# An expert backbone on one core: up matrices in runs of 8192 bytes, token rows stored in the order of the gather

## The chip, the cores and the metric

The kernel runs on one core of one Trainium2 chip. The metric is the device time of one execution in microseconds (us). Three runs of the kernel before are given, with their median; beside them stands one execution that was profiled.

The engines are called by the names of the profile: PE (TensorE, with PEld for its loads of the stationary operand), DVE (VectorE), ACT (ScalarE), POOL (GpSimd) and SP (SyncE, which here only issues transfers). One core has 16 DMA engines.

## What is computed

Two layers of a diffusion backbone on 256 latent and 256 context tokens of width 1024, all in float32. Each layer has a mixer (Fourier mixing, differential attention, a recurrent unit), and then a mixture of 32 experts, of which each token takes two. The change lies in the experts:

```python
def _hier_moe(xt, w_group, b_group, w_router, b_router, w1, w3, w2):
    # w1, w3: (32, 1024, 512), w2: (32, 512, 1024)
    ...                                  # group, then the two best experts of the group
    def body(acc, blk):
        e, toks, ws = blk
        xb = xpad[toks]
        hb = jax.nn.silu(xb @ w1[e]) * (xb @ w3[e])
        yb = (hb @ w2[e]) * ws[:, None].astype(xb.dtype)
        return acc.at[toks].add(yb), None

for l in range(DEPTH):                   # DEPTH = 2
    ...                                  # x (and in layer 0 also the context) through the mixer
    hx2 = _adaln(x, norm2_g[l], sh2, sc2).reshape(B * S, D)
    y = _hier_moe(...)                   # layer 0: 512 tokens; layer 1: the 256 latent ones
    x = x + g2 * y.reshape(B, S, D)
```

Every expert is loaded in full in either layer: 2 MB each of w1, w3 and w2, so 192 MB a layer.

## The kernel before

A token tile has 128 tokens: four tiles in layer 0, two in layer 1. For each layer `mixer` and `proj_prep` run, and then `moe`. The order of the instructions on each engine is the order in which the code is written.

**Loads.** All weights go through one list, `stream`, from which `issue` (L169) takes the next load, gets a slot `S()` of 128 x 2048 floats (22 of them) and issues the transfer on SP (L177). `issue` is called as slots come free; SP then waits for the slot's last reader. A load of an expert is half a matrix, 1 MB: for w1 and w3 512 rows of 512 floats, for w2 256 rows of 1024. `pairs` (L194) puts two neighbouring rows side by side in a partition:

```python
return ap.rearrange("(j p i) f -> p j (i f)", p=128, i=2)
```

For w2 there is one `j`, so that a partition gets 2 x 1024 floats in one piece, 8192 bytes. For w1 and w3 there are two, each of 2 x 512 floats: two pieces of 4096 bytes that lie 128 x 4096 bytes apart in memory. The experts go in units: a unit is one expert with up to 64 tokens, or two experts with up to 32 each. The loads of a unit come in the order w1 and w3 of the first half, w1 and w3 of the second, w2. The first three experts (18 loads) are fixed and are loaded ahead; for the others SP reads the expert's number from the routing (L222).

**Token rows.** `stage_a` to `stage_d` of `proj_prep` make a tile's normed rows in `buf` (128 tokens x 1024 channels): `stage_a` on DVE and ACT, with a small operation on POOL (L162) for the root, `stage_b` on DVE (L1166, two operations of 512 elements), `stage_c` on PE with copies on ACT (transposes, and the logits of the routing). `stage_d` (L1183) splits the rows into two parts for the gather: ACT casts them to `hh` (L1189), POOL subtracts (L1190) to get the rest, `hl`. The order written out is: `stage_d` of the tile before the last follows `stage_b` of the last. Behind the last `stage_c` stands the routing, a chain of small DVE operations from L1235 on, which ends in the one-hot tables (L1386).

**Gather and experts.** `gather` (L1393) multiplies `hh` and `hl` as stationary operands with the one-hot tables, and so gets the tokens of a unit with channels on partitions. Since a partition of a w1 load holds rows 2m and 2m + 1 of a block of 256, the stationary operand must be every second channel: `hsl` (L1373) takes it through `odd` (L1369), with a step of two floats. `up` (L1446) multiplies with w1 and w3, `act` makes the hidden values, `hid_t` transposes them, `down` (L1470) multiplies with w2, `combine` (L1485) brings the result back to the tokens. `overflow` with `block` (L1498) is for tokens that don't fit in the units; it runs a loop whose count comes from the routing.

Of the kernel before, what the change touches and what calls it, by code (L numbers as in the profile page):

```python
# [17 lines left out]
D = 1024  # L18
# [51 lines left out]
def tile_backbone(  # L70
# [27 lines left out]
    V, A, G, PE, SP = nc.vector, nc.scalar, nc.gpsimd, nc.tensor, nc.sync  # L98
# [19 lines left out]
    def f(ap):  # L118
        return ap.bitcast(FT)
# [35 lines left out]
    ident = ca[:, IDENT:IDENT + 128]  # L155
# [9 lines left out]
    stream = []  # L165
# [3 lines left out]
    def issue(n):  # L169
        while state["issued"] < min(n, len(stream)):  # L170
            key, src, kk = stream[state["issued"]]
            if callable(src):
                src = src()
            t = S()
            dst = t[:, 0:2048].rearrange("p (k f) -> p k f", k=kk)
            for i, one in enumerate(src if isinstance(src, list) else [src]):
                SP.dma_start(dst[:, i * one.shape[1]:(i + 1) * one.shape[1]], one)  # L177
            loaded[key] = t
            state["issued"] += 1

# [10 lines left out]
    def kp(ap):  # L191
        return ap.rearrange("(k p) f -> p k f", p=128)

    def pairs(ap):  # L194

        return ap.rearrange("(j p i) f -> p j (i f)", p=128, i=2)

    def s_mod(l, n):
        for h in range(2):
# [17 lines left out]
    def expert(l, rank, w):  # L217

        if rank < FIXED[l]:
            return w[l, rank]  # L220
        if (l, rank) not in picked:
            picked[l, rank] = nc.values_load(  # L222
                by_rank[l][0:1, rank:rank + 1], engines=(ET.SP,), min_val=0, max_val=NE - 1,
                skip_runtime_bounds_check_because="the ranks are a permutation of the experts")
        return w[l, bass.DynSlice(picked[l, rank], 1)].rearrange("o a f -> (o a) f")

    def s_exp(l, ranks):
        for h in range(2):
            for e in ranks:
                stream.append((("w1", l, e, h), lambda e=e, h=h: pairs(expert(l, e, w1)[h * 512:(h + 1) * 512, :]), 2))  # L230
                stream.append((("w3", l, e, h), lambda e=e, h=h: pairs(expert(l, e, w3)[h * 512:(h + 1) * 512, :]), 2))
        for h in range(2):
            for e in ranks:
                stream.append((("w2", l, e, h), lambda e=e, h=h: pairs(expert(l, e, w2)[h * 256:(h + 1) * 256, :]), 1))

    def s_experts(l):
        at = len(stream)
# [824 lines left out]
    def proj_prep(l, mixh, mixl, raw, pre, ends):  # L1062
# [34 lines left out]
        ws = dict(enumerate(pre))  # L1097
# [45 lines left out]
        hh, hl = [], []  # L1143
        buf = S()
# [38 lines left out]
        def stage_d(i):  # L1183

            o = slice(i % 2 * D, (i % 2 + 1) * D)
            if i % 2 == 0:
                hh.append(S(FR))
                hl.append(S(FR))
            A.copy(hh[i // 2][:, o], buf[:, o])  # L1189
            G.tensor_sub(hl[i // 2][:, o], buf[:, o], f(hh[i // 2][:, o]))  # L1190

        for i in range(nt):
            p = pz[i] if l else PS()
# [65 lines left out]
        for i in range(2):  # L1259
            m = c1[2 + i]  # L1260
# [13 lines left out]
        key, rank = scratch(32), scratch(32)  # L1274
# [87 lines left out]
    def moe(l, r):  # L1362
        tts, nt, hh, hl = r["tts"], r["nt"], r["hh"], r["hl"]
# [5 lines left out]
        def odd(ap, k):  # L1369

            return ap.rearrange("p (j m i) -> p j m i", m=128, i=2)[:, k // 2, :, k % 2]

        def hsl(t, i, d):  # L1373
            return odd(t[i // 2][:, (i % 2) * D:(i % 2 + 1) * D], d)

        ohs, xts, wss, ots = {}, {}, {}, {}

# [120 lines left out]
        def block(rc, wc, ws, tiles):  # L1498
            o, ot, y1, s0, s1, x2, x3, pa, pb, pd = tiles
            y0 = o  # L1500
            for i in range(nt):
                ov = o[:, i * 128:(i + 1) * 128].rearrange("p (b h s) -> p b h s", b=2, h=2)
                for h in range(2):
                    V.tensor_tensor(out=ov[:, :, h], in0=iota[:, None, :].to_broadcast([128, 2, 32]),
                                    in1=rc[:, h, i:i + 1][:, :, None].to_broadcast([128, 2, 32]), op=OP.is_equal)
            spin(BS[0], hh[0], pb)

            n = 0
            for i in range(nt):
                for t in (hh, hl):  # L1510
                    for h in range(2):
                        c = (i % 2) * D + h * 512
                        mm((pa, pd)[h], o[:, i * 128:(i + 1) * 128], t[i // 2][:, c:c + 512],
                           n == 0, n == 2 * nt - 1)
                    n += 1
            A.copy(s0[0:64, :], pa[0:64, :])
            V.tensor_copy(s0[64:128, :], pd[64:128, :])
            spin(BS[1], hh[0], pb)
            for k in range(4):
                PE.transpose(pd[:, k * 128:(k + 1) * 128], odd(s0, k), ident)  # L1520
                if k == 1:
                    A.copy(s1[:, 0:256], pd[:, 0:256])
            V.tensor_copy(s1[:, 256:512], pd[:, 256:512])
            up(0, lambda k: s1[:, (k % 4) * 128 + (k // 4) * 64:(k % 4) * 128 + (k // 4 + 1) * 64], [ws], pa)
            for i in range(nt):
                PE.transpose(pb[:, i * 128:(i + 1) * 128], f(o[:, i * 128:(i + 1) * 128]), ident)
            spin(BS[2], hh[0], pd)
            for h in range(2):
                c = slice(h * 256, (h + 1) * 256)
                A.activation(s0[0:64, c], pa[0:64, c], AF.Silu)  # L1530
                V.tensor_mul(s0[0:64, c], s0[0:64, c], pa[64:128, c])
                for k in (2 * h, 2 * h + 1):
                    PE.transpose(pd[:, k * 64:(k + 1) * 64], odd(s0[0:64, :], k), ident[0:64, 0:64])
            A.copy(s1[:, 0:256], pd[:, 0:256])
            V.tensor_copy(ot[:, 0:nt * 128], pb[:, 0:nt * 128])
            down(s1, [ws], pa[0:64, :], pa[64:128, :])
            spin(BS[3], hh[0], pd)

            for h, y in enumerate((y0, y1)):
                a = 64 * h  # L1540
                A.copy(y[a:a + 64, :], pa[a:a + 64, :])
                V.tensor_sub(y[64 - a:128 - a, :], pa[a:a + 64, :], f(y[a:a + 64, :]))
            xs = s0, s1, x2, x3
            for n in range(2 * nt):
                h, i = n // nt, n % nt
                tt, p, t = tts[i], (pb, pd, pa)[n % 3], xs[n % 4]
                mm(p, ot[:, i * 128:(i + 1) * 128], (y0, y1)[h], True, True)
                c = slice(h * 512, (h + 1) * 512)
                gg = (D if tt < 2 else 0) + h * 512
                V.scalar_tensor_tensor(t, p, wc[:, 0, i:i + 1], g2[:, gg:gg + 512], op0=OP.mult, op1=OP.mult)  # L1550
                ADD(n, 2 * nt).tensor_add(xr_(tt, c), xr_(tt, c), t)

        def overflow():
# [3 lines left out]
            with tc.If(v > 0):  # L1557
# [21 lines left out]
                ws = {k: [S(), S()] for k in ("w1", "w3", "w2")}  # L1579
# [3 lines left out]
                with tc.For_i(0, v, 1):  # L1583

                    V.reduce_max(top, rem, axis=AX.X)
                    V.tensor_tensor(out=one, in0=rem, in1=top.to_broadcast([128, 32]), op=OP.is_equal)
                    V.tensor_tensor(out=one, in0=one, in1=t32, op=OP.mult)
                    V.reduce_max(code, one, axis=AX.X)
                    V.tensor_tensor(out=one, in0=t32, in1=code.to_broadcast([128, 32]), op=OP.is_equal)
                    V.tensor_scalar(top, code, -1.0, 32.0, op0=OP.mult, op1=OP.add)  # L1590
                    V.tensor_copy(eid, top[0:1])
                    e = nc.values_load(eid, engines=(ET.SP,), min_val=0, max_val=NE - 1,
                                       skip_runtime_bounds_check_because="the place of a maximum among the experts")
                    for key, w, rows, kk in (("w1", w1, 512, 2), ("w3", w3, 512, 2), ("w2", w2, 256, 1)):
                        for h in range(2):
                            SP.dma_start(ws[key][h].rearrange("p (k f) -> p k f", k=kk),
                                         pairs(w[l, bass.DynSlice(e, 1)].rearrange("o a f -> (o a) f")[h * rows:(h + 1) * rows, :]))
                    for o, a in ((rc, rme), (wc, wte)):
                        V.tensor_tensor(out=prod, in0=a, in1=oneb, op=OP.mult)
                        V.reduce_sum(o[:, 0], prod, axis=AX.X)  # L1600
                    V.tensor_scalar(rc[:, 1], rc[:, 0], -32.0, None, op0=OP.add)
                    V.scalar_tensor_tensor(rem, one, -64.0, rem, op0=OP.mult, op1=OP.add)
                    V.scalar_tensor_tensor(rme, oneb, -64.0, rme, op0=OP.mult, op1=OP.add)
                    block(rc, wc, ws, tiles)
# [191 lines left out]
```

## Time and profile before

| | us |
|---|---|
| runs (3): median, lowest, highest | 1519.53, 1518.34, 1521.59 |
| the profiled execution, whole | 1518.4 |
| its span in the trace | 1516.5 |
| PE busy | 1301.8 (86%) |
| PEld busy | 684.3 (45%) |
| DVE busy | 617.9 (41%) |
| ACT busy | 366.1 (24%) |
| POOL busy | 360.0 (24%) |

Times within the trace count from the start of the span. Layer 0 runs to about 820 us, its experts from about 341 us; layer 1's experts run from about 1044 us to the end. A slice of the page is 37.9 us. [...]

### The profile page before, as it was taken

Reading aid. Unit: us, or ns where it says so; the run is one execution under the profiler, and the core shown is the slowest. Engines: PE = TensorE matmul, PEld = TensorE weight load, DVE = VectorE, ACT = ScalarE, POOL = GpSimd, SP = SyncE. Lnnn points to the kernel's source line nnn. Section 1 sums busy time; section 2 is a strip of 40 time slices with the busy share of each in tenths; the row PEclk is TensorE's granted clock in tenths of the full one; section 3 lists DMA queues with packets and bytes.
Section 4 is the critical chain, followed back from the end, with each engine's and each line's share of the span. In section 5 each row is a group of like instructions: output and inputs, shape, how many; then the busy total and the mean of one; then the engine's idle time right before and its main releaser. Section 6 shows DMA issues by size and latency. Waiting matters only on the chain. (4 is left out here: it accounts for less than half of the span.)

```text
span 1516.5 us, 18764 instructions
## 1 busy us (share of the span) xinstructions
PE 1301.8 (86%) x6910; PEld 684.3 (45%) x6910; DVE 617.9 (41%) x1209; ACT 366.1 (24%) x757; POOL 360.0 (24%) x396
## 2 busy tenths in 40 slices
PE   5989987969999897989898999787989878897775
PEld 3767544755545352535352776375334223231221
DVE  3587586562343322232223678875122111110111
ACT  3433664322111010101012544741111001010000
POOL 2333012420252222222222651141111111100110
PEclk9999999989999998999998999998999989889898
DMA  9943362275999999999999924184999999999996
GB/s 340 388 149 121 116 220 76 84 305 235 413 414 410 414 412 413 412 414 412 413 412 389 376 86 139 37 336 187 412 414 413 413 414 411 413 414 413 413 413 253
DMA packets 134266, 489.66 MB, mean 323 GB/s; under 512 B 10411, under 2 KB 13081, under 8 KB 117785
## 3 DMA queue, kind: packets, MB, share of 16 engines
q1 hardware_dynamic: 129520, 485.11, 81.1%
q10 hardware_dynamic: 4649, 3.29, 0.9%
q8 instruction: 56, 0.92, 0.2%
q14 instruction: 41, 0.34, 0.1%
HBM read 487.32 MB, written 1.05 MB: 322 GB/s over the span
## 5 line engine op out<-in xcount | busy, mean ns | idle before, releaser
L125 PE MATMUL ps<-s 128*32 128x512 f32 (+3 forms) x2488 | 532.7, 615 | 92.3 <-DMA s<-in_w 88.3
L125 PEld LDWEIGHTS ps<-s 128*32 128x32 f32 (+2 forms) x2488 | 173.4, 138 | 409.1 <-issue 222.2
L1496 POOL TENSOR_TENSOR xres<-xres,w 128x512 f32<-128x512 f32 x92 | 116.4, 1292 | 429.1 <-DVE w L1495 429.1
L1460 DVE SCALAR_TENSOR_TENSOR w<-w,ws,ps 64x512 f32<-64x512 f32 x48 | 35.9, 747 | 413.6 <-ACT w L1459 413.6
L125 PE MATMUL ps<-s,ht 128*32 128x512 f32 (+1 forms) x1056 | 178.8, 596 | 8.9 <-ACT ht L1467 7.2
L125 PE MATMUL ps<-w,s 128*128 128x512 f32 x672 | 168.9, 404 | 1.3 <-POOL w L526 0.6
L1459 ACT ACTIVATE w<-ps 64x512 f32<-64x512 f32 x48 | 28.4, 592 | 569.0 <-PE ps L125 569.0
L1496 POOL TENSOR_TENSOR s<-s,w 128x512 f32<-128x512 f32 x50 | 63.2, 1287 | 373.5 <-DVE w L1495 373.5
L125 PEld LDWEIGHTS ps<-w,s 128*128 128x128 f32 x672 | 127.6, 193 | 34.2 <-issue 4.4
L526 POOL TENSOR_TENSOR w<-s,w 128x512 fp32r<-128x512 f32 x80 | 110.4, 1391 | 122.2 <-ACT w L525 104.8
L1495 DVE TENSOR_TENSOR w<-ps,s 128x512 f32<-128x512 f32 x148 | 91.0, 681 | 71.3 <-PE ps L125 71.2
L125 PE MATMUL ps<-s,w 128*128 128x512 f32 (+2 forms) x480 | 101.3, 361 | 6.0 <-DVE s L519 3.2
L125 PEld LDWEIGHTS ps<-s,ht 128*32 128x32 f32 (+1 forms) x1056 | 50.7, 122 | 114.0 <-issue 99.6
L125 PE MATMUL ps<-w 128*128 128x512 f32 (+1 forms) x392 | 89.9, 381 | 2.5 <-ACT w L1481 1.4
L125 PEld LDWEIGHTS ps<-s,w 128*128 128x128 f32 x480 | 75.5, 198 | 35.3 <-issue 12.3
L1482 DVE TENSOR_TENSOR w<-ps,w 128x512 fp32r<-128x512 f32 x48 | 30.9, 686 | 135.2 <-ACT w L1481 135.2
L125 PE MATMUL ps<-oh,s 128*128 128x256 f32 (+1 forms) x640 | 84.0, 293 | 0.0
L125 PEld LDWEIGHTS ps<-oh,s 128*128 128x128 f32 x640 | 81.6, 205 | 3.2 <-issue 2.4
L125 PEld LDWEIGHTS ps<-w 128*128 128x128 f32 x392 | 67.1, 197 | 35.2 <-issue 18.0
L125 PE MATMUL ps<-s,cond 128*32 128x512 f32 x336 | 55.4, 645 | 0.0
L1408 DVE COPY s<-ps 128x512 f32<-128x512 f32 (+1 forms) x26 | 16.9, 649 | 93.2 <-PE ps L125 93.2
L525 ACT CAST w<-s 128x512 fp32r<-128x512 f32 x80 | 48.3, 620 | 4.3 <-issue 1.4
(260 smaller groups left out, 1131.7 us busy)
## 6 DMA issues: line engine op xcount, KB each, us to landing
s<-in_w SPq DMA_DIRECT2D x384, 1024.0 KB, 19.4
s<-in_w_mod SPq DMA_DIRECT2D x48, 1024.0 KB, 12.7
s<-in_w_in SPq DMA_DIRECT2D x18, 1024.0 KB, 14.9
s<-in_w_out SPq DMA_DIRECT2D x8, 512.0 KB, 6.6
s<-in_w_out SPq DMA_DIRECT2D x4, 1024.0 KB, 7.9
s<-in_const_b SPq DMA_DIRECT2D x2, 768.0 KB, 14.8
s<-in_xc SPq DMA_DIRECT2D x2, 512.0 KB, 4.7
xres<-in_x SPq DMA_DIRECT2D x2, 512.0 KB, 8.0
```

What stands on the lines that cost most here:

```text
L125: PE.matmul(o, l, r, start=start, stop=stop)
L525: A.copy(wh[:, 0:n], src)
L526: G.tensor_sub(wl[:, 0:n], src, f(wh[:, 0:n]))
L1408: (V.tensor_copy if dd % 2 else A.copy)(v3(xt[:, dd * 512:(dd + 1) * 512], 256)[:, :, 0:m * 128], v3(ps, 256)[:, :, 0:m * 128])
L1459: A.activation(sh[a:a + 64, :], ps[a:a + 64, :], AF.Silu)
L1460: V.scalar_tensor_tensor(sh[a:a + 64, :], sh[a:a + 64, :], ws, ps[64 - a:128 - a, :], op0=OP.mult, op1=OP.mult)
L1482: V.tensor_sub(yl, ps, f(yh))
L1495: V.tensor_tensor(out=t, in0=ps, in1=g2[:, gg:gg + 512], op=OP.mult)
L1496: (V if end and h else G).tensor_add(xr_(tt, c), xr_(tt, c), t)
```

## The change

`pairs` gives way to `runs`: a partition gets four neighbouring rows of w1 or w3, 8192 bytes in one piece. For w2 the result is what it was. For the up matrices channel `4m + i` of a half then sits in partition m, at place i. `stage_d` therefore writes `hh` and `hl` in that order: for each half of 512 channels first all m with i = 0, then i = 1, and so on. It reads `buf` with a step of four floats and writes without a step, and it does so in two casts and two subtractions for a tile where there was one of each. `hsl` takes 128 neighbouring floats. The hidden values still use `odd`, since w2 lies as before. In `block`, the gathered rows come in the new order, so that their transposes need no step.

```diff
-            dst = t[:, 0:2048].rearrange("p (k f) -> p k f", k=kk)
+            dst = t[:, 0:2048].rearrange("p (k f) -> p k f", k=kk) if kk else t[:, 0:2048]
...
-                SP.dma_start(dst[:, i * one.shape[1]:(i + 1) * one.shape[1]], one)
+                SP.dma_start(dst[:, i * one.shape[1]:(i + 1) * one.shape[1]] if kk else dst, one)
...
-    def pairs(ap):
-
-        return ap.rearrange("(j p i) f -> p j (i f)", p=128, i=2)
+    def runs(ap):
+
+        return ap.rearrange("(p i) f -> p (i f)", p=128)
...
-                stream.append((("w1", l, e, h), lambda e=e, h=h: pairs(expert(l, e, w1)[h * 512:(h + 1) * 512, :]), 2))
+                stream.append((("w1", l, e, h), lambda e=e, h=h: runs(expert(l, e, w1)[h * 512:(h + 1) * 512, :]), 0))
...
-            A.copy(hh[i // 2][:, o], buf[:, o])
-            G.tensor_sub(hl[i // 2][:, o], buf[:, o], f(hh[i // 2][:, o]))
+            b4 = buf[:, o].rearrange("p (h m i) -> p h i m", h=2, i=4)
+            h4, l4 = [t[i // 2][:, o].rearrange("p (h i m) -> p h i m", h=2, i=4) for t in (hh, hl)]
+            for h in range(2):
+                A.copy(h4[:, h], b4[:, h])
+                G.tensor_sub(l4[:, h], b4[:, h], f(h4[:, h]))
...
         def hsl(t, i, d):
-            return odd(t[i // 2][:, (i % 2) * D:(i % 2 + 1) * D], d)
+            a = (i % 2) * D + d * 128
+            return t[i // 2][:, a:a + 128]
...
-                PE.transpose(pd[:, k * 128:(k + 1) * 128], odd(s0, k), ident)
+                PE.transpose(pd[:, k * 128:(k + 1) * 128], s0[:, k * 128:(k + 1) * 128], ident)
```

The lines for w3 and w2 in `s_exp`, and the loads in `overflow`, change like that of w1.

On SP, the second unit's loads of layer 0 stand so before (a name with a number is a buffer, `in_w1` and the like are the matrices in memory):

```order
L177 DMA s_2742<-in_w1 128x2x1024
L177 DMA s_2744<-in_w3 128x2x1024
L177 DMA s_2746<-in_w1 128x2x1024
L177 DMA s_2748<-in_w3 128x2x1024
L177 DMA s_2750<-in_w2 128x2048
L177 DMA s_2752<-in_w2 128x2048
```

and so in the changed kernel:

```order
L177 DMA s_2750<-in_w1 128x2048
L177 DMA s_2752<-in_w3 128x2048
L177 DMA s_2754<-in_w1 128x2048
L177 DMA s_2756<-in_w3 128x2048
L177 DMA s_2758<-in_w2 128x2048
L177 DMA s_2760<-in_w2 128x2048
```

The order is the same; the up matrices' transfers have the shape of w2's.

On POOL, at the end of layer 0's `proj_prep` (`n2r` holds the roots of a tile, `s_2473` and `s_2614` the parts `hl`, `s_2391` is `buf`), before:

```order
L1190 TENSOR_TENSOR s_2473<-s_2391,s_2472 128x1024
L162 TENSOR_TENSOR n2r_2192<-n2r_2192,ca_72 128x1 x2
L1190 TENSOR_TENSOR s_2614<-s_2391,s_2613 128x1024 x2
L1496 TENSOR_TENSOR s_70<-s_70,w_3027 128x512
L1496 TENSOR_TENSOR s_70<-s_70,w_3033 128x512
```

and in the changed kernel:

```order
L1193 TENSOR_TENSOR s_2473<-s_2391,s_2472 128x512 x2
L162 TENSOR_TENSOR n2r_2192<-n2r_2192,ca_72 128x1 x2
L1193 TENSOR_TENSOR s_2618<-s_2391,s_2617 128x512 x4
L1500 TENSOR_TENSOR s_70<-s_70,w_3035 128x512
L1500 TENSOR_TENSOR s_70<-s_70,w_3041 128x512
```

Nothing moved past anything else; each subtraction became two of half the size, and on ACT each cast likewise.

## Rows read from the trace of the kernel before

**Rows 1.** The page: GB/s of 40 slices; shares of the chain of waits, by engine.

```profile
GB/s 340 388 149 121 116 220 76 84 305 235 413 414 410 414 412 413 412 414 412 413 412 389 376 86 139 37 336 187 412 414 413 413 414 411 413 414 413 413 413 253
...
PE 19%; DMA 18%; DVE 4%; ACT 2%; issue 1%; POOL 1%; SPq 0%; DVEq 0%; ACTq 0%; POOLq 0%
```

**Rows 2.** Table of stretches: stretch, length, busy us (instructions) by engine, clock, DMA share, GB/s.

```profile
360.00:520.00 160.00, 154.08 (x916) 72.87 (x916) 55.22 (x89) 23.05 (x48) 50.36 (x40) 1.00 1.02 411
...
520.00:815.00 295.00, 263.94 (x1452) 120.69 (x1456) 76.92 (x131) 34.82 (x75) 70.16 (x57) 0.95 1.02 412
...
1060.00:1500.00 440.00, 361.80 (x1927) 125.19 (x1928) 71.01 (x131) 42.19 (x93) 49.66 (x40) 0.92 1.02 412
```

**Rows 3.** Table of stretches, loads of w2 alone: the highest and the lowest rate.

```profile
1201.00:1207.00 6.00, 6.00 (x38) 1.66 (x32) 0.74 (x1) 0.59 (x1) 0.00 (x0) 1.00 1.02 423
...
1292.00:1298.00 6.00, 5.50 (x25) 1.34 (x26) 0.00 (x0) 0.00 (x0) 0.00 (x0) 0.50 1.01 416
```

**Rows 4.** Table of stretches, loads of w1 and w3 alone: the highest and the lowest rate.

```profile
628.00:642.00 14.00, 13.52 (x78) 6.63 (x78) 6.72 (x11) 1.55 (x3) 9.93 (x8) 1.00 1.03 411
...
1136.00:1151.00 15.00, 14.48 (x74) 5.55 (x67) 3.77 (x6) 1.49 (x4) 4.22 (x4) 1.00 1.02 407
```

**Rows 5.** DMA traffic of 1201 to 1207, 628 to 642, 357 to 800, 1060 to 1502.

```profile
DMA packets 347, 2.54 MB, mean 423 GB/s; under 512 B 37, under 2 KB 37, under 8 KB 37
...
DMA packets 1493, 5.75 MB, mean 411 GB/s; under 512 B 91, under 2 KB 91, under 8 KB 1492
...
DMA packets 39990, 182.46 MB, mean 412 GB/s; under 512 B 2772, under 2 KB 2772, under 8 KB 32701
...
DMA packets 39566, 181.37 MB, mean 410 GB/s; under 512 B 2768, under 2 KB 2768, under 8 KB 32118
```

**Rows 6.** Expert loads by tile, issue to landing: 357 to 815, then 1060 to 1502.

```profile
DMA to landing us min/median/max: 7.0/19.4/20.7
...
DMA to landing us min/median/max: 6.1/20.0/21.2
```

**Rows 7.** PE's waits (total us, times, longest): 370 to 860, then 1040 to 1516.

```profile
PE ps L125 <- DMA s<-in_w: 27.5, 17, 6.8
...
PE ps L125 <- DMA s<-in_w: 62.4, 53, 4.6
```

**Rows 8.** Timeline of PE (start, us, work, [idle before]): last waits of both layers.

```profile
798.29 1.04 PE L125 MATMUL ps<-s 128*32 128x512 f32 x2 [1.40 <-DMA s<-in_w]
...
800.84 1.08 PE L125 MATMUL ps<-s 128*32 128x512 f32 x4 [1.50 <-DMA s<-in_w]
...
1502.20 1.06 PE L125 MATMUL ps<-s,ht 128*32 128x512 f32 x8 [0.81 <-DMA s<-in_w]
```

**Rows 9.** Timelines of POOL and DVE, end of `proj_prep` in layers 0 and 1.

```profile
317.39 2.34 POOL L1190 TENSOR_TENSOR s<-s 128x1024 fp32r<-128x1024 f32 x1
...
317.42 2.85 DVE L1166 SCALAR_TENSOR_TENSOR s<-s,n2r 128x512 f32<-128x512 f32 x1 [0.66 <-POOL n2r L162]
...
320.20 0.74 DVE L1166 SCALAR_TENSOR_TENSOR s<-s,n2r 128x512 f32<-128x512 f32 x1
...
1031.66 0.34 DVE L1248 TENSOR_TENSOR w<-w 128x8 f32<-128x8 f32 x1
...
1032.03 0.17 DVE L1249 TENSOR_TENSOR w<-w,ca 128x8 f32<-128x8 f32 x1
```

**Rows 10.** Groups by shape: total us, mean ns of one, idle before them.

```profile
L1189 ACT CAST s<-s 128x1024 fp32r<-128x1024 f32 x6 | 6.3, 1043 | 0.0
...
L1115 ACT CAST s<-s 128x512 fp32r<-128x512 f32 x16 | 9.3, 621 | 0.0
...
L1496 POOL TENSOR_TENSOR xres<-xres,w 128x512 f32<-128x512 f32 x92 | 116.4, 1292 | 429.1 <-DVE w L1495 429.1
...
L125 PEld LDWEIGHTS ps<-oh,s 128*128 128x128 f32 x640 | 81.6, 205 | 3.2 <-issue 2.4
...
L125 PEld LDWEIGHTS ps<-w,s 128*128 128x128 f32 x672 | 127.6, 193 | 34.2 <-issue 4.4 <-POOL w L526 1.4 <-POOL s L904 0.8
```

More of the change, by code (lines that the diff above doesn't have):

```diff
@@ L229, in s_exp @@
             for e in ranks:
-                stream.append((("w1", l, e, h), lambda e=e, h=h: pairs(expert(l, e, w1)[h * 512:(h + 1) * 512, :]), 2))
-                stream.append((("w3", l, e, h), lambda e=e, h=h: pairs(expert(l, e, w3)[h * 512:(h + 1) * 512, :]), 2))
+                stream.append((("w1", l, e, h), lambda e=e, h=h: runs(expert(l, e, w1)[h * 512:(h + 1) * 512, :]), 0))
+                stream.append((("w3", l, e, h), lambda e=e, h=h: runs(expert(l, e, w3)[h * 512:(h + 1) * 512, :]), 0))
         for h in range(2):
             for e in ranks:
-                stream.append((("w2", l, e, h), lambda e=e, h=h: pairs(expert(l, e, w2)[h * 256:(h + 1) * 256, :]), 1))
+                stream.append((("w2", l, e, h), lambda e=e, h=h: runs(expert(l, e, w2)[h * 256:(h + 1) * 256, :]), 0))
     def s_experts(l):
@@ L1593, in overflow @@
                                        skip_runtime_bounds_check_because="the place of a maximum among the experts")
-                    for key, w, rows, kk in (("w1", w1, 512, 2), ("w3", w3, 512, 2), ("w2", w2, 256, 1)):
+                    for key, w, rows in (("w1", w1, 512), ("w3", w3, 512), ("w2", w2, 256)):
                         for h in range(2):
-                            SP.dma_start(ws[key][h].rearrange("p (k f) -> p k f", k=kk),
-                                         pairs(w[l, bass.DynSlice(e, 1)].rearrange("o a f -> (o a) f")[h * rows:(h + 1) * rows, :]))
+                            SP.dma_start(ws[key][h][:, 0:2048],
+                                         runs(w[l, bass.DynSlice(e, 1)].rearrange("o a f -> (o a) f")[h * rows:(h + 1) * rows, :]))
                     for o, a in ((rc, rme), (wc, wte)):
```

## The prediction

> **What bounds the kernel now.** I read the page's slices first: from the eleventh slice to the twenty-first, and again from the twenty-ninth to the thirty-ninth, the DMA moves 410 to 414 GB/s in every slice, and nowhere else does it for long [rows 1]. These are the two expert stages, one per layer. The chain of waits says the same of layer 1 (it can't be followed back into layer 0, which is why its shares make half of the span): 18% of the span is DMA beside 19% TensorE [rows 1]. Then the table of stretches: the mean share of the DMA engines is 1.02 from 360 to 815 us and from 1060 to 1500 us, while TensorE (PE) has 31 us to spare in the 295 us after 520 and 78 in the 440 us after 1060 [rows 2]. In 360 to 520 us PE is busy 154 of 160 us, so there alone it keeps pace with the DMA. So both expert stages are as long as their bytes take, and what counts is the rate.
>
> That rate isn't one number. Twelve short stretches in which nearly all packets are of 8192 bytes (the down matrices w2) run at 416 to 423 GB/s, with a mean by length of 419.8; the highest and the lowest are shown [rows 3]. Fourteen stretches in which all packets are of 4096 bytes (w1 and w3) run at 407 to 411, mean 409.3; again the highest and the lowest are shown [rows 4]. That they are what I call them is seen in the packet counts: in 1201 to 1207 us only 37 of 347 packets are under 8 KB, and these 37 are the small ones under 512 B; in 628 to 642 us 1492 of 1493 are under 8 KB, 1401 of them above 2 KB [rows 5]. The engines are full in both (share 1.02 and 1.03), so the difference of 2.6% is what a longer packet is worth. It can't be that something else waits.
>
> **The change part by part.** (1) The up matrices. A load of 1 MB went as 256 packets of 4096 bytes and will go as 128 of 8192, 8 KB in a row to each partition. A load of w2 is already just that, 1 MB in one piece and 8 KB to a partition, by the same queue, from the same memory, so I take its rate for the new one. What is affected are the 4 KB packets inside the two full stretches: 32701 - 2772 = 29929 from 357 to 800 us, and 32118 - 2768 = 29350 from 1060 to 1502 us [rows 5]. That is 122.6 MB and 120.2 MB. At 409.3 GB/s they take 299.5 and 293.7 us, at 419.8 GB/s 292.0 and 286.4: **7.5 us less in layer 0 and 7.3 in layer 1, 14.8 together.** The first 18 loads of either layer, which come before the stretches, meet idle engines and save nothing. Bounds: with the worst of one kind and the best of the other (411 against 416) 3.6 + 3.5 = 7.1 us, with 409.3 against 423 9.7 + 9.5 = 19.2 us. I take the means, since they rest on 67 and 205 us.
>
> Does the gain reach the end? In layer 1 PE waits for expert loads 53 times and 62.4 us in all [rows 7], the last time at 1502 us for the last load [rows 8], so the end moves with the DMA. In layer 0 it waits 17 times, 27.5 us [rows 7], and the last two waits, 1.4 and 1.5 us for up matrices, end at 798.3 and 800.8 us, at the last up products of the layer [rows 8]. The end of PE's row is the latest of (landing + the work behind it) over all loads; the last wait binds now, and every wait before it has the later waits as slack, 2.9 us and more, against a gain that differs by 0.017 us for each microsecond between them. So the whole 7.5 us should come through. The queue must not run dry either: the shortest time from issue to landing is 7.0 us in layer 0 and 6.1 in layer 1, the median 19.4 and 20.0 [rows 6]. Around 440 us, where the 7.0 stands, the DMA will be ahead by only about 1.4 us. The small loads of layer 1's projections follow in the same queue and shift along with it.
>
> (2) The token rows' parts. Each of the six calls of `stage_d` (four tiles in layer 0, two in layer 1) makes two casts on ScalarE (ACT) and two subtractions on GpSimd (POOL) of 512 elements, reading with a step of 16 bytes, where one of 1024 without a step stood. No row of before has such a step on either engine. What it touches is VectorE (DVE): before the last tile of layer 0, POOL's subtraction (2.34 us from 317.39) and DVE's L1166 start together, and L1166 takes 2.85 us, where its next one takes 0.74 [rows 9]; it waits until POOL is done. This pair of L1166, 2.85 + 0.74 = 3.6 us less a small overlap, so 3.5, is on the way to the routing, the first gather, and so to the moment at which expert loads flow freely. In layer 1 the same happens, and there a small DVE operation, L1248, also waits until the last subtraction ends (0.34 us, where the next of its kind takes 0.17) [rows 9].
>
> Let h be the time of one half on POOL. The nearest rows are 1.17 us (half of 2.34) and 1.29 us (a 512-element addition on POOL without a step) [rows 10]; the far end is 2.34, as if the step doubled each element's time. The pair now ends 2.34 us (POOL) and some 1.2 us of its own work after the start. If DVE and POOL take turns, it ends at 2h + 1.2, so 2h - 2.3 us later than now; if DVE gets both of its operations through after the first half, h - 2.3. The last subtraction of a layer can start after a cast of 0.62 us instead of 1.04 [rows 10], and ends 2h - 2.34 - 0.42 = 2h - 2.8 us later than now; so L1248 moves back by nothing for h up to 1.4, and by 1.9 us for 2.34. Over both layers that is -2.4 us at best, +0.5 for 1.29 with turns, and 2 x (2.4 + 1.9) = +8.6 at the far end. I take 0, by the nearer rows, and keep both ends. If ACT's casts doubled too, POOL would start some 0.4 us later, another +0.8.
> [...]
>
> (3) The gather reads its weights without a step. Its 640 weight loads take 205 ns each, others of that shape 193 [rows 10]; they lie beside matmuls, and only the two first gathers (64 and 32 loads) are on the path. 96 x 12 ns = 1.2 us at most; I take 0. The overflow block, which is edited too, isn't executed: no row of its lines is in the trace.
>
> Sum: -14.8 + 0 + 0. The profiled execution took 1518.4 us, 1516.5 of them its span, so 1503.6 by its clock; it lies 1.1 us below the median of the runs, 1519.5, so **1504.7 us**.
>
> **The rivals.**
> - The 8 KB rate is only that of bursts. A w2 phase lasts about 10 us, between phases of 4 KB packets. If a steady stream of 8 KB packets gains 1.2% (416 against 411), 7.1 us go: 1512.4 us. For it: the lowest of the twelve stretches. Against it: the other eleven.
> [...]
> - Layer 0 is bound by PE as soon as the DMA is 2.5% faster, and only layer 1 gains: 1519.5 - 7.3 = 1512.2 us. For it: PE is busy 154 of 160 us up to 520 us. Against it: 27.5 us of waits for loads, nearly four times what is to be gained.
> - The rate belongs to w2 and not to the packet's length; the change then does nothing: 1519.5 us. Against it: the pieces of memory are alike.
> - Slower: reading with the step on POOL costs so much that DVE's last `stage_b` and its routing wait for it in both layers. With turns both places together cost 2 x (2h - 2.3 + 2h - 2.8) = 8h - 10.2 us. It eats the gain at h = 3.1 us, and makes the kernel slower by more than 3 us from h = 3.5, three times the present time per element; h = 4 gives 1519.5 - 14.8 + 21.8 = 1526.5 us.
>
> **How the numbers follow.** The forecast gets 0.75 (1499 to 1510), the burst 0.10, layer 0 bound by PE 0.08, nothing 0.04, slower 0.03. About 0.2%, 3 us, is what a measurement of this kernel can tell from no change. Faster: 0.75 + 0.10 + 0.08 = 0.93; same 0.04; slower 0.03. The low end is the 19.2 us of the best rates less some of the 2.4 of part 2, about 1499; the high end, 1513, takes in the two cases of one half of the gain and the forecast with the far price of the step (8.6 us).
>
> **What would show it.** Right: no packets of 4 KB in the expert stages, a rate near 420 GB/s from 360 to 800 us and through all of layer 1's stage, both stages about 7 us shorter, fewer PE waits in layer 0, L1166 of the last tile at 2.5 to 3.8 us for its two. Wrong: a rate near 413 with 8 KB packets (burst); the right rate but gaps in the DMA share between 420 and 520 us (PE-bound); POOL's halves at over 2 us, and L1166's pair over 6.

## The result and the profile after

The changed kernel takes 1504.5 us in the median (1502.9 to 1505.8), the kernel before beside it 1519.4. The medians differ by 14.8 us, 1.0%. The ratio is 0.9899, with a 95% interval from 0.9887 to 0.9912, which is 13.4 to 17.2 us. The profiled execution took 1505.1 us, 1503.3 of them its span. It lies 0.6 us above its median, the one of before 1.0 below the 1519.4, so the two traces differ by 13.2 us and not by 14.8.

The page after, GB/s of the 40 slices, the packets, and the shares of the chain of waits:

```profile
GB/s 346 388 151 120 119 207 93 85 305 204 421 421 405 421 420 421 420 421 421 420 421 386 383 91 136 34 312 186 420 420 420 421 421 420 421 421 421 421 421 244
DMA packets 101498, 489.66 MB, mean 326 GB/s; under 512 B 10411, under 2 KB 13081, under 8 KB 52249
...
DMA 25%; PE 13%; DVE 4%; ACT 2%; issue 1%; POOL 1%; SPq 0%; DVEq 0%; ACTq 0%; POOLq 0%
```

In the eleventh to the twenty-first slice and the twenty-ninth to the thirty-ninth, the DMA now moves 420 or 421 GB/s where it moved 410 to 414 [rows 1], with one exception, the 405 of the thirteenth. In the chain, which again reaches back only into layer 1, the DMA has passed TensorE: 25% and 13%, where it was 18% and 19% [rows 1].

The table of stretches (length; busy us and instructions of each engine; granted clock, DMA share, GB/s), as in [rows 2]:

```profile
360.00:520.00 160.00, 154.14 (x917) 72.84 (x916) 55.27 (x89) 23.32 (x49) 49.91 (x40) 1.00 1.00 415
520.00:815.00 295.00, 264.01 (x1472) 121.58 (x1472) 84.92 (x140) 35.82 (x77) 73.51 (x59) 0.97 1.01 419
1060.00:1480.00 420.00, 346.59 (x1860) 120.08 (x1860) 70.31 (x130) 40.86 (x90) 49.71 (x40) 0.92 1.01 421
```

The DMA traffic of layer 0's expert stage, then of layer 1's, as in [rows 5]:

```profile
DMA packets 25012, 182.37 MB, mean 418 GB/s; under 512 B 2769, under 2 KB 2769, under 8 KB 2769
...
DMA packets 24840, 180.95 MB, mean 417 GB/s; under 512 B 2768, under 2 KB 2768, under 8 KB 2768
```

"Under 2 KB" and "under 8 KB" are the same number: no packet of 4096 bytes is left, and 22243 of 8192 carry all but 0.2 MB of layer 0's stage.

Where the time went is read from three moments of each layer. Of after, on DVE and PE (start, us, work, idle before it): the last tile's first L1166 in layer 0, the first gather, the last wait for an up matrix; then the same three in layer 1, where the last wait is for a w2:

```profile
315.81 2.11 DVE L1166 SCALAR_TENSOR_TENSOR s<-s,n2r 128x512 f32<-128x512 f32 x1 [0.66 <-POOL n2r L162]
341.44 0.56 PE L125 MATMUL ps<-oh,s 128*128 128x256 f32 x1
793.72 0.76 PE L125 MATMUL ps<-s 128*32 128x512 f32 x4 [1.44 <-DMA s<-in_w]
...
1017.64 2.12 DVE L1166 SCALAR_TENSOR_TENSOR s<-s,n2r 128x512 f32<-128x512 f32 x1 [0.68 <-POOL n2r L162]
1038.87 0.56 PE L125 MATMUL ps<-oh,s 128*128 128x256 f32 x1
1488.98 0.64 PE L125 MATMUL ps<-s,ht 128*32 128x512 f32 x4 [0.79 <-DMA s<-in_w]
```

Of before, the two first gathers and layer 1's L1166 (the others stand in [rows 8, 9]):

```profile
341.34 0.56 PE L125 MATMUL ps<-oh,s 128*128 128x256 f32 x1
...
1023.67 2.87 DVE L1166 SCALAR_TENSOR_TENSOR s<-s,n2r 128x512 f32<-128x512 f32 x1 [0.68 <-POOL n2r L162]
1044.33 0.56 PE L125 MATMUL ps<-oh,s 128*128 128x256 f32 x1
```

| stretch | before, us | after, us | difference |
|---|---|---|---|
| start to the last tile's L1166, layer 0 | 317.42 | 315.81 | -1.6 |
| L1166 to the first gather, layer 0 (`stage_d`, routing) | 23.92 | 25.63 | +1.7 |
| first gather to the last up matrix, layer 0 | 459.50 | 452.28 | -7.2 |
| from there to L1166, layer 1 (rest of layer 0, mixing) | 222.83 | 223.92 | +1.1 |
| L1166 to the first gather, layer 1 | 20.66 | 21.23 | +0.6 |
| first gather to the last w2, layer 1 | 457.87 | 450.11 | -7.8 |
| from there to the end | 14.30 | 14.32 | 0.0 |

The two expert stages gave 15.0 us. The two stretches with `stage_d` took 2.3 back. The first and the fourth stretch, which the change hardly touches, differ by -1.6 and +1.1; that they differ from trace to trace anyway is seen in the same kernel run again (below), where the L1166 of layer 0 starts at 319.50 instead of 315.81.

### The profile page after: what moved, and what is told of

Read it like the earlier page. It is cut to its first block, busy times and chain, and to the rows that moved or that the text cites. A ratio compares the mean times of both kernels' runs of the same rounds, so it can differ in the third digit from the quotient of the medians.

```text
span 1503.3 us, 18776 instructions
## 1 busy us (share of the span) xinstructions
PE 1295.8 (86%) x6910; PEld 683.5 (45%) x6910; DVE 623.1 (41%) x1209; ACT 372.7 (25%) x763; POOL 364.8 (24%) x402
## 5 line engine op out<-in xcount | busy, mean ns | idle before, releaser
L125 PE MATMUL ps<-s,w 128*128 128x512 f32 (+2 forms) x480 | 104.7, 369 | 5.2 <-DVE s L519 2.4
```

Of the source, the lines that this page charges most:

```text
L125: PE.matmul(o, l, r, start=start, stop=stop)
```

## What was tried

**Is it the packet's length?** Three kernels cut the loads otherwise. In the first, every load of w1 and w3 goes as two DMAs with the same bytes to the same places:

```diff
+    def cut(ap):
+        t = ap.rearrange("(p j i) f -> p j (i f)", p=128, j=2)
+        return [t[:, 0:1], t[:, 1:2]]
...
-                stream.append((("w1", l, e, h), lambda e=e, h=h: runs(expert(l, e, w1)[h * 512:(h + 1) * 512, :]), 0))
+                stream.append((("w1", l, e, h), lambda e=e, h=h: cut(expert(l, e, w1)[h * 512:(h + 1) * 512, :]), 2))
...
```

> The changed kernel, but each load of w1 and w3 goes as two DMAs of 512 KB with packets of 4096 bytes; the bytes, their places, the order of the loads and the token rows' parts stay. Theory (what counts is the length of the packet): the 59279 packets of 4 KB are back, the stretches run at 407 to 411 GB/s again, and the time is 1504.5 + 14.8 = 1519.3 us. Whatever it lies above or below the kernel before is then the price of the parts' new order, 1.7 us in layer 0 and 0.6 to 1.3 in layer 1 by the two traces: 1519.4 + 2.3 to 3.0 = 1521.7 to 1522.4 us, if nothing drifts. Rival (the gain comes from the rows' order in memory or from the gather and not from the packet's length): 1504.5 us and 420 GB/s. Twice as many issues on SP should cost nothing, since SP waits for free buffers most of the time.

It took 1524.2 us, 1.0026 times before (1.0015 to 1.0036), and 19.7 us more than the changed kernel. The rows of the two stretches:

```profile
520.00:815.00 295.00, 260.52 (x1440) 119.44 (x1444) 79.78 (x134) 35.18 (x76) 73.08 (x59) 0.96 1.02 412
1066.00:1500.00 434.00, 360.96 (x1884) 122.14 (x1884) 70.29 (x130) 40.86 (x90) 49.68 (x40) 0.90 1.02 413
```

412 and 413 GB/s are, within one, the rates of before [rows 2]: the rows' order in memory and the gather have no part in the gain. The time is above the 1521.7 to 1522.4 that the price of the parts allowed; what the twice as many DMAs cost is asked below.

The second cuts the loads of w2 in the same way and leaves the up matrices alone.

> The changed kernel, but each load of w2 goes as two DMAs of 512 KB with packets of 4096 bytes; w1 and w3 keep their runs of 8192. Theory (the rate goes with the length of the packet, whichever matrix): the 7289 + 7448 packets of 8 KB of w2 in the two stretches, 120.7 MB, go at 409.3 instead of 419.8 GB/s: 294.9 instead of 287.5 us, 7.4 us more, 1511.9 us; stretches of w2 alone at 407 to 411. Rival (the rate belongs to w2, wherever it lies and however it is cut): 1504.5 us, w2 at 420.

1514.6 us, 0.9972 times before (0.9960 to 0.9984). A stretch of w2 alone, and its packets:

```profile
1199.00:1204.00 5.00, 5.00 (x30) 1.23 (x24) 0.00 (x0) 0.48 (x1) 0.00 (x0) 0.76 1.03 410
...
DMA packets 563, 2.05 MB, mean 410 GB/s; under 512 B 63, under 2 KB 63, under 8 KB 563
```

w2 in packets of 4096 bytes runs at 410 GB/s, where it ran at 416 to 423 in 8192 [rows 3]. So the rate doesn't belong to the matrix. The time is again above what the packets explain, by 2.7 us.

The third goes down to 2048 bytes, with plainly stored parts:

```diff
-                stream.append((("w1", l, e, h), lambda e=e, h=h: runs(expert(l, e, w1)[h * 512:(h + 1) * 512, :]), 0))
+                stream.append((("w1", l, e, h), lambda e=e, h=h: kp(expert(l, e, w1)[h * 512:(h + 1) * 512, :]), 4))
...
-            for h in range(2):
-                A.copy(h4[:, h], b4[:, h])
-                G.tensor_sub(l4[:, h], b4[:, h], f(h4[:, h]))
+            A.copy(hh[i // 2][:, o], buf[:, o])
+            G.tensor_sub(hl[i // 2][:, o], buf[:, o], f(hh[i // 2][:, o]))
...
```

> w1 and w3 go with packets of 2048 bytes (a partition holds every 128th row), the token rows' parts are stored plainly and the gather reads them without a step, so that neither side pays for a permutation. Theory (a packet costs a fixed time beside its bytes: 4096 bytes at 409.3 GB/s are 160.1 ns of one of 16 engines, 8192 at 419.8 are 312.2, so 152.1 ns for each 4096 bytes and 8.0 ns fixed): 2048 bytes take 84.1 ns, 389.9 GB/s; the 242.8 MB of the two stretches take 622.7 us where the changed kernel takes 578.4, 44.3 more, less 2.3 to 3.0 us for the plain parts: about 1546 us. If the rate of the 2 KB loads of layer 1's mixing matrices (377 GB/s from 815 to 862 us in the trace after) holds instead: 644 us, 65.6 more, about 1567 us. Rival (each halving costs the same 2.5%, 399 GB/s): 30.1 more, about 1532 us.

1553.5 us, 1.0223 times before (1.0208 to 1.0238). Two stretches in which the loads' packets are of 2048 bytes, and the DMA traffic of the second (none of its 3315 packets has 8 KB):

```profile
718.00:733.00 15.00, 14.52 (x86) 6.77 (x82) 6.31 (x10) 1.55 (x3) 9.93 (x8) 1.00 1.04 387
1251.00:1268.00 17.00, 12.86 (x40) 2.50 (x40) 1.46 (x4) 0.37 (x1) 0.00 (x0) 0.60 1.05 387
...
DMA packets 3315, 6.58 MB, mean 387 GB/s; under 512 B 101, under 2 KB 101, under 8 KB 3315
```

387 GB/s, as in nearly all such stretches of this trace. At that rate a packet of 2048 bytes takes 84.7 ns of one of the 16 engines; from the longer ones the fixed time of 8.0 ns had given 84.1. The equal loss at each halving, 399 GB/s, is out. With 387 the two stretches take 627 us where the changed kernel's take 578: 49 us more, and 49.0 were measured. The 2 to 3 us that the plain parts should have saved don't show in that sum; in this trace layer 0 takes 25.56 us from L1166 to the first gather, as long as with the new order.

**What do more DMAs cost?** Both kernels with pieces lay above the sum. The plainest test is the kernel before with each up load in two DMAs, packets as they were:

```diff
+    def apart(ap):
+        t = pairs(ap)
+        return [t[:, 0:1], t[:, 1:2]]
...
-                stream.append((("w1", l, e, h), lambda e=e, h=h: pairs(expert(l, e, w1)[h * 512:(h + 1) * 512, :]), 2))
+                stream.append((("w1", l, e, h), lambda e=e, h=h: apart(expert(l, e, w1)[h * 512:(h + 1) * 512, :]), 2))
...
```

> The kernel before, with each load of w1 and w3 issued as two DMAs of 512 KB; packets stay at 4096 bytes, rows, places and the parts' order stay as before the change. Theory (a further DMA brings 16 small packets and about 21 ns on each engine): 231 further DMAs in the two stretches, 4.9 us more, 1524.1 us. Then of the 1524.2 us of the changed kernel with 4096-byte pieces next to nothing is left for the parts' new order, and its 19.7 us over the changed kernel are 14.8 of packet length and 4.9 of further DMAs. Rival (the further DMAs are free, and the parts' order costs the 4.9 us): 1519.2 us.

1521.6 us, 1.0015 times before (1.0006 to 1.0024): 2.3 us more by the ratio and 1.4 by the medians (1520.2 for before beside it), half of what was expected or less, and not nothing. By the ratios, the changed kernel with 4096-byte pieces lies 4.0 us above before. So about 2.3 of them are the DMAs and 1.7 the new order of the parts, the first known to 1.4 us, the second, a difference of two, to some 2.

For 8192-byte packets the first way of asking was no good: a load was split into partitions 0 to 63 and 64 to 127.

```diff
+    def halves(ap):
+        t = runs(ap)
+        return [t[0:64], t[64:128]]
...
```

> The changed kernel, but each load of w1 and w3 goes as two DMAs of 64 partitions each, still with packets of 8192 bytes: twice as many DMAs as in the changed kernel, the same number as where the up matrices went in two 512 KB pieces of 4096-byte packets. Theory (each further DMA brings 16 small packets, about 21 to 24 ns on each of the 16 engines, which is what is left over of the two runs with pieces: 4.85 us by 231, 2.7 us by 115): 1504.5 + 4.9 = 1509.4 us, and the difference to the run with 4096-byte pieces, 1524.2, is the packet's length alone, 14.8. Rival (the further DMAs cost nothing, and the rest is the rows' or the packets' doing): 1504.5 us.

2223.4 us. That is no price of a DMA. A hundred microseconds of layer 0's stage, as table of stretches and as DMA traffic:

```profile
500.00:600.00 100.00, 71.03 (x312) 28.59 (x312) 11.91 (x22) 8.02 (x17) 9.89 (x8) 0.77 0.99 230
...
DMA packets 3383, 23.05 MB, mean 230 GB/s; under 512 B 573, under 2 KB 573, under 8 KB 573
```

The engines are full (share 0.99) and move 230 GB/s with packets of the same 8192 bytes: each takes 1.8 times as long as at 420. The next kernel gave one DMA the even and the other the odd partitions:

```diff
+    def turns(ap):
+        t = runs(ap)
+        return [t[0::2], t[1::2]]
...
```

> The changed kernel, each load of w1 and w3 as two DMAs, one to the even partitions and one to the odd ones, packets of 8192 bytes. It puts the question again that the loads to partitions 0 to 63 and 64 to 127 could not answer, as those ran at 220 to 250 GB/s. [...] Rival (64 rows in one DMA are slow wherever they lie): about 230 GB/s and some 2200 us again.

1510.5 us, 0.9940 times before (0.9924 to 0.9955), where 1504.5 with the 4.9 us at which the further DMAs had been put makes 1509.4, and in the rows the full rate:

```profile
520.00:790.00 270.00, 242.55 (x1364) 116.24 (x1368) 76.24 (x129) 33.76 (x73) 70.22 (x56) 0.96 1.01 420
```

So loads into 64 partitions in a row ran at 230 GB/s, and loads into 64 spread over all at 420; why, no run shows. The doubled DMAs cost 4.6 to 6 us here by the medians (against 1505.9 and 1504.5 for the changed kernel), and 2.3 with packets of 4096 bytes. That the two prices differ isn't shown: the intervals of the ratios here (0.9940 against 0.9905 for the changed kernel beside it) leave some 2 to 9 us. Nor do these runs tell the price of a further DMA from that of every second partition.

**What does the new order of the parts cost, and what does it buy?** The loads of 8192 bytes with the parts stored plainly, the step on the gather's side:

```diff
...
-            a = (i % 2) * D + d * 128
-            return t[i // 2][:, a:a + 128]
+            return t[i // 2][:, (i % 2) * D:(i % 2 + 1) * D].rearrange("p (h m i) -> p h m i", h=2, i=4)[:, d // 4, :, d % 4]
...
```

`stage_d` is again as before the change, as in the kernel with 2048-byte packets.

> The changed kernel's loads, but the token rows' parts are stored plainly, by one cast and one subtraction of 1024 elements as before, and the gather's weight loads read them with a step of 16 bytes. Theory (the parts' new order costs 1.7 us in layer 0 and 0.6 to 1.3 us in layer 1, and TensorE's weight loads don't mind the step): 1504.5 - 2.3 to 3.0 = 1501.5 to 1502.2 us, POOL's subtraction 2.35 us for 1024 again, L1166's pair 3.5 us. Rival A (as predicted, the new order costs nothing on the path): 1504.5 to 1505.7 us, with up to 1.2 us for the two first gathers. Rival B (a step of 16 bytes costs the weight loads half as much again, 193 to 290 ns): 96 loads of the first gathers by 97 ns, 9.3 us more less the 2.3 to 3.0: about 1511 us.

1520.7 us, 1.0010 times before (1.0001 to 1.0019): all of the gain is gone. My theory falls. Rival B has the mechanism, but only about half of the price, 9.3 us of the 18 to 19 that the step costs: it counted the first gathers alone. The gather's weight loads and matmuls by shape (total us, mean ns of one), of this kernel:

```profile
L125 PEld LDWEIGHTS ps<-oh,s 128*128 128x128 f32 x640 | 151.1, 330 | 3.2 <-issue 2.4
L125 PE MATMUL ps<-oh,s 128*128 128x256 f32 x544 | 130.6, 402 | 0.0
```

and of the changed one:

```profile
L125 PEld LDWEIGHTS ps<-oh,s 128*128 128x128 f32 x640 | 81.1, 202 | 3.2 <-issue 2.4
L125 PE MATMUL ps<-oh,s 128*128 128x256 f32 x544 | 72.4, 296 | 0.0
```

A step of 16 bytes makes a weight load 330 ns instead of 202; a step of 8 bytes had made it 205 [rows 10]. The matmuls behind the loads go from 296 to 402 ns. And now the table shows what becomes of layer 0, with PE's waits for loads under it:

```profile
440.00:460.00 20.00, 19.48 (x91) 7.58 (x88) 3.35 (x6) 2.04 (x4) 1.64 (x2) 1.00 0.82 310
...
PE ps L125 <- DMA s<-in_w: 4.9, 5, 1.3
```

PE hardly waits for a load any more (4.9 us, after: 23.6), and the DMA has gaps: 310 GB/s at a share of 0.82. TensorE has become the bound in layer 0. The whole loss lies there, from this layer's first gather to L1166 of layer 1, here 692.40 us and in the changed kernel 676.20:

```profile
342.97 0.56 PE L125 MATMUL ps<-oh,s 128*128 128x256 f32 x1
...
1035.37 2.88 DVE L1166 SCALAR_TENSOR_TENSOR s<-s,n2r 128x512 f32<-128x512 f32 x1 [0.67 <-POOL n2r L162]
```

The other way round, the step was put on the writes of `stage_d`: casts and subtractions read the tile in order and write every element 512 bytes from the last.

```diff
-            b4 = buf[:, o].rearrange("p (h m i) -> p h i m", h=2, i=4)
-            h4, l4 = [t[i // 2][:, o].rearrange("p (h i m) -> p h i m", h=2, i=4) for t in (hh, hl)]
+            b4 = buf[:, o].rearrange("p (h m i) -> p h m i", h=2, i=4)
+            h4, l4 = [t[i // 2][:, o].rearrange("p (h i m) -> p h m i", h=2, i=4) for t in (hh, hl)]
```

> The changed kernel, but the step lies on the other side: the casts read the normalized tile without a step and write with one of 512 bytes, into the same places; the subtractions read the tile without a step, read the cast's result with 512 and write with 512. Theory (a step costs only where it is read): the casts go back to 0.62 us a half, POOL has one of its two reads with a step and takes 1.2 to 1.6 us a half; 1503 to 1504.5 us. Rival (each element of its own costs as much on the writing side): casts of 1.1 us, POOL at 1.6 us or more a half, 1504.5 us or above.

1505.2 us, 0.9902 times before (0.9887 to 0.9917). The groups of `stage_d` by shape, of this kernel and, behind it, of the changed one:

```profile
L1193 POOL TENSOR_TENSOR s<-s 128x512 fp32r<-128x512 f32 x12 | 19.2, 1619 | 14.4 <-ACT s L1192 14.3
L1192 ACT CAST s<-s 128x512 fp32r<-128x512 f32 x12 | 12.1, 1110 | 0.0
```

```profile
L1193 POOL TENSOR_TENSOR s<-s 128x512 fp32r<-128x512 f32 x12 | 19.3, 1630 | 14.5 <-ACT s L1192 14.4
L1192 ACT CAST s<-s 128x512 fp32r<-128x512 f32 x12 | 12.7, 1113 | 0.0
```

1110 against 1113 ns for a cast, 1619 against 1630 for a subtraction: for the cast it doesn't matter on which side the elements are apart. A subtraction costs as much with a step on one of its reads and on its write as with a step on the other read alone.

The last one divides the step between the two sides. `stage_d` keeps two neighbouring channels side by side, so that it reads 8 of every 16 bytes, and the gather takes every second float, as before the change:

```diff
-            b4 = buf[:, o].rearrange("p (h m i) -> p h i m", h=2, i=4)
-            h4, l4 = [t[i // 2][:, o].rearrange("p (h i m) -> p h i m", h=2, i=4) for t in (hh, hl)]
+            b4 = buf[:, o].rearrange("p (h m a b) -> p h a m b", h=2, a=2, b=2)
+            h4, l4 = [t[i // 2][:, o].rearrange("p (h a m b) -> p h a m b", h=2, a=2, b=2) for t in (hh, hl)]
...
-            a = (i % 2) * D + d * 128
-            return t[i // 2][:, a:a + 128]
+            return odd(t[i // 2][:, (i % 2) * D:(i % 2 + 1) * D], d)
...
```

> The changed kernel's loads; the token rows' parts are stored so that two neighbouring channels stay side by side (the casts and the subtractions read 8 bytes and step 16), and the gather's weight loads read with a step of 8 bytes, as before the change. Theory (what the step costs goes with the 16-byte pieces touched, two elements from each instead of one): casts of 0.62 to 0.87 us a half and subtractions of 1.2 to 1.4, so 1 to 3 us less than the changed kernel, 1501.5 to 1503.5 us, with weight loads at 205 ns. Rival (a broken run costs the same however short the step): casts of 1.1, subtractions of 1.6 us a half and 1504.5 us.

1502.6 us, 0.9896 times before (0.9881 to 0.9910). Its groups:

```profile
L125 PEld LDWEIGHTS ps<-oh,s 128*128 128x128 f32 x640 | 82.1, 206 | 3.2 <-issue 2.4
L1193 POOL TENSOR_TENSOR s<-s 128x512 fp32r<-128x512 f32 x12 | 16.2, 1376 | 12.1 <-ACT s L1192 12.1
L1192 ACT CAST s<-s 128x512 fp32r<-128x512 f32 x12 | 7.3, 659 | 0.0
```

A cast of 659 ns is nearly the 621 of a half without a step [rows 10], a subtraction of 1376 is near the 1292 of such an addition, and the weight loads are where they were before the change. From L1166 to the first gather it takes 23.62 us in layer 0 and 19.54 in layer 1 (after: 25.63 and 21.23). So these runs fit a price that goes with the number of elements that are taken from each 16 bytes: one was slow (1113 ns for a cast), two nearly as fast (659) as four (621). The three engines agree here, POOL less sharply (1630 to 1376 ns) than ACT (1113 to 659) and the weight loads (330 with one float of each 16 bytes, 206 with two, 202 with four).

Once more, this kernel and the changed one side by side:

> The kernel that keeps pairs of channels side by side once more, beside the changed kernel on the same chip. Theory (the parts' order costs the changed kernel 1.7 us in layer 0 and 0.6 in layer 1, and pairs cost nothing): 2.3 us below the changed kernel, 1502.2 us. Rival (what the order costs is taken up by later waits): 1504.5 us.

> The changed kernel itself, for the comparison with the one that keeps pairs: 1504.5 us.

1503.9 us (0.9893 times before, 0.9878 to 0.9908) and 1505.9 us (0.9905, 0.9890 to 0.9920). The difference is 2.0 us, and 1.9 by the medians given further up (1502.6 and 1504.5); the intervals overlap, so the times alone don't prove it. From L1166 to the first gather it takes 24.55 us in layer 0 and 19.54 in layer 1 with pairs, 25.33 and 21.11 without. The two moments of layer 1, with pairs and without:

```profile
1019.05 1.78 DVE L1166 SCALAR_TENSOR_TENSOR s<-s,n2r 128x512 f32<-128x512 f32 x1 [0.67 <-POOL n2r L162]
1038.59 0.56 PE L125 MATMUL ps<-oh,s 128*128 128x256 f32 x1
...
1019.54 2.11 DVE L1166 SCALAR_TENSOR_TENSOR s<-s,n2r 128x512 f32<-128x512 f32 x1 [0.67 <-POOL n2r L162]
1040.65 0.56 PE L125 MATMUL ps<-oh,s 128*128 128x256 f32 x1
```

The same stretch in the traces of all these kernels, by the order of the parts:

| parts | traces | layer 0, us | layer 1, us |
|---|---|---|---|
| plain (before, and three variants) | 4 | 23.92 to 25.56 | 20.00 to 20.66 |
| new order (after, again, and five variants) | 7 | 23.36 to 25.65 | 21.05 to 21.23 |
| pairs kept | 2 | 23.62, 24.55 | 19.54, 19.54 |

In layer 1 the three orders stand apart in every trace: the new one costs about 1 us (at least 0.4), and the kernels with pairs are 1.5 us and more below it. In layer 0 the ranges overlap, so there one pair of traces proves neither a price nor a gain. I take the kernel that keeps pairs as the better one, by some 0.13%.

## Why the prediction came out right, point by point

**The rate.** Both stages bound by the DMA, 14.8 us to be had, 7.5 and 7.3: the table gives 7.2 and 7.8, 15.0 together. That 8192-byte packets would run in a steady stream as they did in w2's short phases was right (420 or 421 in every full slice of layer 1). The fixed time per packet, of which the forecast made no use (8.0 ns, an estimate from 409.3 and 419.8 GB/s), holds down to 2048 bytes: 84.1 ns a packet by it, 84.7 at the 387 GB/s measured.

**That it reaches the end.** After the change PE waits for loads 17 times, 23.6 us in all, in layer 0, and 50 times, 58.3 us, in layer 1:

```profile
PE ps L125 <- DMA s<-in_w: 23.6, 17, 5.5
...
PE ps L125 <- DMA s<-in_w: 58.3, 50, 5.3
```

They hardly shrank, in layer 0 from 27.5 to 23.6 us with as many waits [rows 7]: DMA still sets the end of both stages. (Fewer waits in layer 0 had been named as a sign of being right; it came in their time and not in their number.) But the place that I had named as tight, around 440 us, did run dry. The stretch there, and the time from issue to landing of the expert loads from 357 to 815 us (least, median, most):

```profile
440.00:460.00 20.00, 19.52 (x126) 8.46 (x126) 11.13 (x16) 2.62 (x5) 10.26 (x8) 1.00 0.96 390
...
DMA to landing us min/median/max: 5.7/19.8/21.4
```

390 GB/s in 20 us are 1.4 us less than at 420, while PE is busy for 19.52 of the 20: that is a bite which TensorE takes out of layer 0. The longer packets alone don't make it. The changed kernel with 4096-byte pieces, which has the rate of before, has such a gap too:

```profile
460.00:470.00 10.00, 10.00 (x74) 5.07 (x67) 0.74 (x1) 1.44 (x3) 0.00 (x0) 1.00 0.98 363
```

No run shows what else does. The rival that made all of layer 0 bound by PE was far off for this change, and came true for the gather with a step.

**The parts' order.** Taken at 0, with ends of -2.4 and +8.6; by the two traces it costs 1.7 + 0.6 = 2.3 us (1.4 + 0.5 in the same kernel again). Over all traces only the 1 us of layer 1 is sure (table above), and the two ratios further up leave 1.7 us, known to some 2. This is the step that was mis-sized, and by two of its terms. POOL and DVE of layer 0, and DVE of layer 1:

```profile
315.85 3.44 POOL L1193 TENSOR_TENSOR s<-s 128x512 fp32r<-128x512 f32 x2
...
317.84 2.00 DVE L1166 SCALAR_TENSOR_TENSOR s<-s,n2r 128x512 f32<-128x512 f32 x1
...
325.02 1.01 DVE L1251 TENSOR_TENSOR w<-w 128x16 f32<-128x16 f32 x1
...
1025.81 1.49 DVE L1251 TENSOR_TENSOR w<-w 128x8 f32<-128x8 f32 x1
```

A half on POOL takes 1.6 us, not 1.17 to 1.29. DVE's two L1166 take turns with POOL's halves, 2.11 and 2.00 us, as I had thought, and the pair ends 0.5 us later than in [rows 9]; its 4.0 us are above the 3.8 that I had named as a sign of being right. (In the kernel with even and odd partitions the other case came in layer 0: DVE got both through after the first half, 2.69 us.) And a cast takes 1.06 to 1.11 us, not 0.62, so that POOL's last subtraction starts no earlier than before and ends later. The small operation behind it (L1251, formerly L1248) takes 1.49 us in layer 1 where it took 0.34, and 1.01 in layer 0 where it took 0.17. In layer 0 pair and L1251 make 1.3 of the 1.7 us, and the rest is a longer wait for the logits. In layer 1 they make 1.7 us, of which 1.1 come back in shorter waits of DVE for PE. The doubled casts stood in the forecast as a remark of 0.8 us, outside the value taken. The nearest rows were rows without a step, and I gave them the whole weight, where no row showed the step itself. The trace has 1.6 us a half, between those rows (1.17 to 1.29) and the far end (2.34), and a price of 2.3 us, between the 0 taken and 8.6.

**The gather.** Weight loads 202 ns instead of 205, so 0 was right for the edit. What I had not seen is what it is for: with four rows to a partition the old way of reading would have cost as much as the packets bring.

**The sum.** 1504.7 was forecast and 1504.5 measured, but the agreement is closer than the steps: -15.0 + 2.3 is -12.7, the traces differ by 13.2, the medians by 14.8. The rest lies in stretches that the change hardly touches and that move by a microsecond or two from one trace to the next, and in how far the traces lie from their medians. That forecast and median meet within 0.2 us is luck. The order's price is within what a range from 1499 to 1513 was meant to hold.

**The rivals.** The burst is out (420 in a steady stream), and with it its 1.2%: from 4096 to 8192 bytes the rate rose by 2.6%. Out is also the rate that belongs to w2 (410 when cut). Slower through POOL would have needed 3.5 us a half.

## What to carry to other kernels

Where a stage is as long as its bytes, read the rate of each packet length from the trace itself, and work out the fixed time of a packet; here 8.0 ns, an estimate from 409.3 and 419.8 GB/s, which is 2.6% from 4096 to 8192 bytes. Here the longer run in memory left the other operand with a step. With one float taken from each 16 bytes it was paid on whichever side it lay (a cast of 1113 ns or a weight load of 330, against 621 and 202 without); with two floats of each 16 bytes on both sides the price was small (a cast 659 ns against 621, a weight load 206 against 202). And where no row shows a step, don't give the nearest rows without one the whole weight; here the truth (1.6 us) lay between them (1.17 to 1.29) and the far end (2.34).

## What the runs showed of the hardware that I had not expected

- TensorE's weight loads mind a step of 16 bytes (330 ns, against 202 without and 205 with 8), and a cast on ScalarE took as long with the step in its reads (16 bytes, 1113 ns) as in its writes (512 bytes, 1110), against 621 without. An estimate: with 422 ns (1043 - 621) for 512 further elements without a step a half has some 200 ns fixed, so that with the step an element takes 1.8 ns instead of 0.8.
- With loads as DMAs into partitions 0 to 63 and 64 to 127 the rate was little over half (230 GB/s at a share of 0.99); with DMAs into every second partition it was whole (420).
- Cutting each of the 256 up loads of 1 MB in two cost 2.3 us (0.9 to 3.6) with 4096-byte packets, and 4.6 to 6 by the medians with 8192-byte packets to even and odd partitions.
